# A planner of engine queues gets three more rounds, ranked by deadlines worked out backwards from a plan

## The chip, the core and the metric

The kernel runs on one core of a Trainium2 chip. Work is spread over TensorE (PE in the rows; PEld is its weight load), VectorE (DVE), ScalarE (ACT), GpSimd (POOL) and SyncE (SP), which here issues every DMA. Each engine takes its instructions in the order in which they were written to its queue, and waits at one whose inputs aren't there. The metric is the device time of one execution in microseconds (us); lower is better.

## What is computed

Two layers (DEPTH = 2) of a diffusion trunk, over 640 tokens: 512 latent ones and 128 of context. In each layer one input projection feeds three branches.

```python
h = _rms(x, p['norm_g']) * (1 + scale) + shift          # shift, scale, gate from silu(c) @ w_mod
proj = h @ p['w_in']
...
o_a = _attend(q, k, v)                                  # A: latent attention, low-rank q and kv
...
o_f, s_f = _gdn_chunk(gq, gk, gv, g[:, :, 0], beta[:, :, 0], s0[:, 0])   # B: gated DeltaNet, forward
o_bw, s_b = _gdn_chunk(fl(gq), fl(gk), fl(gv), ...)     #    and backward, summed; 4 heads
...
o_c = _chunk_mlp(cu, cv, p)                             # C: 128-position spatial gating
br = jnp.stack([o_a * jax.nn.silu(z_a), o_b * jax.nn.silu(z_b), o_c * jax.nn.silu(z_c)], axis=2)
yb = jnp.einsum('btnw,nwd->btnd', br, p['w_branch'])
y = jnp.sum(gates * yb, axis=2) @ p['w_o']
x = x + gate * y
```

Branch B needs, for each head and direction, the inverse of a 128x128 unit triangular matrix in each chunk of tokens, and then a scan over the chunks.

## The kernel before

Activations lie feature-major, 128 rows by 640 tokens, handled in halves of 320 columns. The long products are made from three matmuls each: weights and activations are split into a rounded part and a rest (`hi` and `lo` of the weights, `hh0` to `hh7` and `hl0` to `hl7` of the normed input), by `split_w` with one copy on ScalarE and one subtraction on VectorE. `dense` runs 24 such matmuls of 320 columns into one of the two PSUM buffers tagged `dn`, and an evacuation on ScalarE or VectorE then empties it.

The layer is written in program order as: the first blocks of the projection (`begin`, `Side`), the decay and gate vectors, and then four DeltaNet heads (`qkv_head`, `gdn_head`, `inverse`), with the projections of other branches between them (`gelu_block`, `silu_block`, `win`); then attention, then the three branches' products (`branch`), then `w_o`. At the start of the kernel the input `xT` is squared and summed for the norm, while the modulation matrix `w_mod` is loaded in 32 pieces into the buffers tagged `G` and multiplied with `s32`.

`inverse` is a chain of small matmuls on PE (tiles `p` of 32x32 and 64x64) with a copy, a transpose or a product on ScalarE or VectorE between each two: `pa`, `t1`, `pb`, `Y2`, `Y2T`, `pc`, `t2`, `pd`, `pe` and so on. Beside `t2`, the copy on which the next small matmuls hang, ScalarE makes twelve quarter copies of `Y2` and `Y2T` into `Y` and `YT` there.

Nothing of this is issued at once. A `Recorder` takes down every instruction with its engine, its predecessors by the tiles that it reads and writes, and a cost in ns from a table (`cost`). `issue` then calls `best`, which plans, and writes the instructions in the planned order; it fixes each engine's order with added dependencies. So every instruction carries the line of `issue` in the profile (L371 before). The planner, `plan`, is a list scheduler: it steps through time, and an engine that is free takes, of the instructions whose inputs are ready, the one with the lowest `prio`, and goes on to the next in rank only if a buffer that it needs isn't free. `prio` is the place in the program (`op.prio = op.n - self.off`), less 100000 for those recorded under `rec.hp()`, such as weight splits, evacuations and softmax. `slack` makes results count as later by so many ns when PE waits for them. `best` tries the four values of `SLACKS` and keeps the plan with the lowest modelled end.

Of the kernel before, what the change touches and what calls it, by code (L numbers as in the profile page):

```python
# [48 lines left out]
HOP = {"V": 36, "S": 36, "G": 60, "PE": 53, "SP": 60}  # L49
AFTER = {"V": 33, "S": 122, "G": 60}  # L50
SLACKS = (0, 60, 120, 180)
ISSUE = 475
DMA_LAG, DMA_RATE = 1900, 340.0

# [5 lines left out]
class Recorder:  # L60
# [94 lines left out]
    def cost(self, op, outs, ins):  # L155
# [3 lines left out]
        if e == "SP":  # L159
            big = max((x.nbytes() if callable(x.nbytes) else x.nbytes) for x in outs + ins)  # L160
            op.occ, op.lat = ISSUE, big / DMA_RATE
        elif e == "PE":
# [17 lines left out]
        else:  # L180
# [22 lines left out]
            if e == "S" and n == 160 and outs[0].ap[0][1] == 32:  # L203
                op.occ, op.lat = 260, 320

    def best(self):

        plans = []
        for slack in SLACKS:
            self.plan(slack)  # L210
            plans.append((self.total, slack))
        return self.plan(min(plans)[1])

    def plan(self, slack):
        import heapq
# [1594 lines left out]
```

## Time and profile before

| | |
|---|---|
| median of 3 runs | 1681.33 us (1680.39 to 1683.24) |
| the profiled execution, its own time | 1683.82 us |
| its span, first to last instruction | 1681.9 us |
| mean granted TensorE clock | 0.989 of full |
| instructions in the profile | 34993 |
| PE / DVE / ACT busy, share of the span | 97% / 76% / 53% |

The span is what the views divide up; 1.9 us of the execution lie around it. A PE that is busy need not be at full rate: it may run at half its clock, and the ends of its matmuls are modelled.

### The profile page before, as it was taken

Reading aid. Unit: us, or ns where it says so; the run is one execution under the profiler, and the core shown is the slowest. Engines: PE = TensorE matmul, PEld = TensorE weight load, DVE = VectorE, ACT = ScalarE, POOL = GpSimd, SP = SyncE. Lnnn points to the kernel's source line nnn. Section 1 sums busy time; section 2 is a strip of 40 time slices with the busy share of each in tenths; the row PEclk is TensorE's granted clock in tenths of the full one; section 3 lists DMA queues with packets and bytes.
Section 4 is the critical chain, followed back from the end, with each engine's and each line's share of the span. In section 5 each row is a group of like instructions: output and inputs, shape, how many; then the busy total and the mean of one; then the engine's idle time right before and its main releaser. Section 6 shows DMA issues by size and latency. Waiting matters only on the chain. (4 is left out here: it accounts for less than half of the span.)

```text
span 1681.9 us, 34993 instructions
## 1 busy us (share of the span) xinstructions
PE 1636.5 (97%) x13286; PEld 1538.7 (91%) x13286; DVE 1284.8 (76%) x3638; ACT 890.2 (53%) x2201; POOL 16.7 (1%) x100
## 2 busy tenths in 40 slices
PE   6999998999999999999999999989999999999998
PEld 5998988999889989989989989989998899899998
DVE  4898898665655768877988987976656557789898
ACT  3566664554545554434445676646545455545453
POOL 0000000000000000000000000000000000000000
PEclk9999999999999999999989999999999999999999
DMA  9312211222121212555542212212211122113342
GB/s 298 95 56 55 62 58 50 66 69 62 46 60 58 91 51 97 178 185 157 188 156 64 58 42 63 58 50 78 70 52 53 49 64 88 57 65 98 94 161 80
DMA packets 94616, 146.39 MB, mean 87 GB/s; under 512 B 14064, under 2 KB 38000, under 8 KB 94448
## 3 DMA queue, kind: packets, MB, share of 16 engines
q1 hardware_dynamic: 94448, 144.15, 28.0%
q8 instruction: 105, 1.72, 0.4%
q14 instruction: 63, 0.52, 0.1%
HBM read 132.28 MB, written 11.83 MB: 86 GB/s over the span
## 5 line engine op out<-in xcount | busy, mean ns | idle before, releaser
L371 PE MATMUL dn<-hh,hi 128*128 128x320 f32 (+1 forms) x1472 | 469.6, 319 | 4.8 <-ACT hh L371 2.1
L371 PE MATMUL dn<-hl,hi 128*128 128x320 f32 (+1 forms) x1472 | 469.1, 319 | 0.4 <-DVE hl L371 0.3
L371 PE MATMUL dn<-hh,lo 128*128 128x320 f32 (+1 forms) x1472 | 467.9, 318 | 0.0
L371 ACT CAST hi<-raw 128x512 fp32r<-128x512 f32 (+1 forms) x300 | 186.1, 620 | 198.5 <-PE dn L371 101.1
L371 PEld LDWEIGHTS dn<-hh,hi 128*128 128x128 f32 (+1 forms) x1472 | 277.1, 188 | 10.1 <-ACT hh L371 3.1
L371 PEld LDWEIGHTS dn<-hl,hi 128*128 128x128 f32 (+1 forms) x1472 | 277.6, 189 | 3.7 <-DVE hl L371 1.2
L371 PEld LDWEIGHTS dn<-hh,lo 128*128 128x128 f32 (+1 forms) x1472 | 277.5, 189 | 2.9 <-issue 1.0
L371 DVE TENSOR_TENSOR lo<-raw,hi 128x512 fp32r<-128x512 f32 (+1 forms) x300 | 206.5, 689 | 60.3 <-ACT hi L371 57.5
L371 PE MATMUL dn<-qkv,hi 128*128 128x320 f32 x768 | 175.0, 313 | 0.5 <-DVE iv L371 0.5
L371 PEld LDWEIGHTS dn<-qkv,hi 128*128 128x128 f32 x768 | 129.4, 189 | 3.3 <-ACT hi L371 1.6
L371 PE MATMUL dn<-qkv,lo 128*128 128x320 f32 x384 | 119.9, 312 | 0.0
L371 ACT CAST hi<-D 128x512 fp32r<-128x512 f32 x88 | 54.6, 623 | 105.9 <-PE dn L371 51.8
L371 PE MATMUL p<-hh,hi 128*128 128x320 f32 x296 | 92.3, 313 | 0.3 <-ACT hi L371 0.3
L371 PE MATMUL p<-hh,lo 128*128 128x320 f32 x296 | 92.2, 312 | 0.0
L371 PE MATMUL p<-hl,hi 128*128 128x320 f32 x296 | 92.0, 311 | 0.2 <-DVE hl L371 0.2
L371 DVE TENSOR_REDUCE mx<-p 128x1 f32<-128x640 f32 x64 | 52.7, 823 | 48.1 <-PE p L371 48.0
L371 ACT ACTIVATE V<-p,mx,scl 128x640 f32<-128x640 f32 x64 | 56.9, 888 | 60.5 <-DVE mx L371 57.2
L371 PEld LDWEIGHTS dn<-qkv,lo 128*128 128x128 f32 x384 | 72.4, 189 | 0.7 <-issue 0.7
L371 PE MATMUL p<-G,hi 128*128 128x320 f32 x286 | 69.3, 308 | 0.0
L371 ACT ACTIVATE th<-dn 128x320 f32<-128x320 f32 x112 | 48.7, 435 | 38.9 <-PE dn L371 38.2
L371 PEld LDWEIGHTS p<-iv,G 32*32 32x32 f32 (+2 forms) x608 | 34.9, 132 | 36.2 <-issue 33.1
L371 PE MATMUL p<-G,G 128*128 128x512 f32 x128 | 65.7, 595 | 0.0
(350 smaller groups left out, 3484.0 us busy)
## 6 DMA issues: line engine op xcount, KB each, us to landing
raw<-in_w_in SPq DMA_DIRECT2D x212, 256.0 KB, 2.7
G<-in_w_mod SPq DMA_DIRECT2D x96, 256.0 KB, 4.4
raw<-in_w_branch SPq DMA_DIRECT2D x48, 256.0 KB, 2.8
D<-in_w_in SPq DMA_DIRECT2D x32, 256.0 KB, 3.3
ld<-sp SPq DMA_DIRECT2D x16, 320.0 KB, 3.1
raw<-in_w_o SPq DMA_DIRECT2D x20, 256.0 KB, 3.1
G<-in_w_uq SPq DMA_DIRECT2D x16, 192.0 KB, 2.7
D<-in_w_o SPq DMA_DIRECT2D x12, 256.0 KB, 3.6
```

The source lines that it names most:

```text
L371: op.ins = getattr(getattr(nc, ENG[op.eng]), op.meth)(*op.args, **op.kw)
```

## The change

`best` now makes 16 plans. For each of the four slacks it plans once with the ranks of before, and then three times more; each further time the rank of an instruction is its deadline in the plan just made. `deadlines` walks that plan from its end to its beginning: an instruction has to be done before the earliest deadline of those that need its result, or that take over its buffer (`slotdeps`), less a hand-over time, and on PE also before the deadline of the next matmul in PE's order. Of the 16 plans the one with the lowest modelled end is issued. Costs, dependencies, buffers and the instructions themselves stay as they are.

```diff
+ROUNDS = 4
...
+    def deadlines(self, out):
+
+        succ = {op.n: [] for op in out}
+        for op in out:
+            for p in op.preds:
+                succ[p].append(op)
+        for op, nm in self.slotdeps:
+            for u in self.users[nm]:
+                succ[u.n].append(op)
+        latest, after = {}, None
+        for op in reversed(out):
+            end = self.total
+            for s_ in succ[op.n]:
+                lag = 53 if s_.eng != op.eng else op.occ - op.lat if op.eng == "PE" else 33
+                end = min(end, latest[s_.n] - lag)
+            t = end - op.lat - (DMA_LAG if op.eng == "SP" else 0)
+            if op.eng == "PE":
+                if after is not None:
+                    t = min(t, latest[after.n] - max(op.occ, op.ld))
+                after = op
+            latest[op.n] = t
+        return latest
+
     def best(self):
 
+
+        first = [op.prio for op in self.ops]
         plans = []
         for slack in SLACKS:
-            self.plan(slack)
-            plans.append((self.total, slack))
-        return self.plan(min(plans)[1])
+            prio = first
+            for n in range(ROUNDS):
+                for op, p in zip(self.ops, prio):
+                    op.prio = p
+                out = self.plan(slack)
+                plans.append((self.total, slack, n, prio))
+                late = self.deadlines(out)
+                prio = [late[op.n] for op in self.ops]
+        _, slack, _, prio = min(plans, key=lambda x: x[:3])
+        for op, p in zip(self.ops, prio):
+            op.prio = p
+        return self.plan(slack)
```

The instructions are the same ones on every engine; their places move by a few up to some tens. On PE the last fifth of the program and the middle of each layer (the branch products) stay in place; what moves lies at the start, in the part of each layer with the DeltaNet heads, and a little at the border of the two layers. Both layers move alike. Three places follow; in the names, the first number is that of the tile.

PE in the inverse of head 0, layer 0, before: `p2_291` are the matmuls `pc`, `p2_293` and `p2_294` are `pd` and `pe`, which read the copy `t2` (`iv_292`), and `dn_443` is the next block of the projection.

```order
L371 MATMUL p2_291_359<-iv_287_355,G_216_284 32x32 x20
L371 MATMUL p2_293_361<-iv_280_348,iv_292_360 32x32 x20
L371 MATMUL p2_294_362<-iv_292_360,iv_280_348 32x32 x10
L371 MATMUL dn_443_511<-hh0_69_137,hi_438_506 128x320
L371 MATMUL dn_443_511<-hl0_70_138,hi_438_506 128x320
L371 MATMUL dn_443_511<-hh0_69_137,lo_439_507 128x320
L371 MATMUL dn_443_511<-hh1_76_144,hi_438_506 128x320
```

The same place on PE now.

```order
L406 MATMUL p2_291_359<-iv_287_355,G_216_284 32x32 x20
L406 MATMUL dn_443_511<-hh0_69_137,hi_438_506 128x320
L406 MATMUL dn_443_511<-hl0_70_138,hi_438_506 128x320
L406 MATMUL dn_443_511<-hh0_69_137,lo_439_507 128x320
L406 MATMUL dn_443_511<-hh1_76_144,hi_438_506 128x320
L406 MATMUL dn_443_511<-hl1_77_145,hi_438_506 128x320
L406 MATMUL dn_443_511<-hh1_76_144,lo_439_507 128x320
L406 MATMUL p2_293_361<-iv_280_348,iv_292_360 32x32 x20
L406 MATMUL p2_294_362<-iv_292_360,iv_280_348 32x32 x10
```

Six dense matmuls moved in between the small ones that make `pc` and those that read its copy.

ACT at this place before, from the copy `t1` (`iv_285`) to the copy `t2` (`iv_292`): `G_288` and `G_289` are `Y`, `iv_290` is `YT`, and `C_424` is the evacuation of the dense buffers `dn_431` and `dn_432`, which comes only after these rows.

```order
L371 COPY G_289_357<-iv_280_348 32x5x32
L371 COPY iv_290_358<-iv_287_355 32x5x32
L371 CAST hi_601_669<-raw_600_668 128x512
L371 COPY iv_290_358<-iv_287_355 32x5x32 x2
L371 COPY G_288_356<-iv_280_348 32x5x32
L371 COPY G_289_357<-iv_280_348 32x5x32
L371 COPY iv_290_358<-iv_287_355 32x5x32
L371 COPY iv_292_360<-p2_291_359 128x160
```

And now, the whole way from `t1` to `t2`.

```order
L406 COPY iv_285_353<-p2_284_352 128x160
L406 ACTIVATE C_422_490<-C_421_489 128x644
L406 COPY C_424_492<-dn_431_499 128x320
L406 COPY G_288_356<-iv_280_348 32x5x32
L406 CAST hi_441_509<-raw_440_508 128x512
L406 COPY G_288_356<-iv_280_348 32x5x32
L406 COPY iv_290_358<-iv_287_355 32x5x32 x4
L406 COPY C_424_492<-dn_432_500 128x192
L406 COPY C_424_492<-dn_432_500 128x128
L406 COPY G_289_357<-iv_280_348 32x5x32
L406 COPY iv_292_360<-p2_291_359 128x160
```

Five quarter copies and a weight split (`hi_601`) moved behind `t2`; the activation `C_422` and three evacuations, which stood behind it, moved ahead of it.

DVE later in layer 0, where the inverse of head 2 begins, before: `iv_728` is the product `Bm` that the first small matmuls (`p2_729`) wait for, `R_727` its factor `brs`; `ir_691`, `res_692`, `br__693`, `br2_694` and `G_701` belong to head 3, whose inverse comes later; `ld_831` empties the dense buffer `dn_830`.

```order
L371 TENSOR_SCALAR D_595_663<-D_595_663,mv_580_648,R_597_665 128x512
...
L371 SCALAR_TENSOR_TENSOR R_727_795<-br2_462_530,c_m01_6_74,R_727_795 128x5
L371 TENSOR_TENSOR ya4_599_667<-ya4_599_667,D_819_887 128x640
L371 SCALAR_TENSOR_TENSOR ir_691_759<-ssq_686_754,r_689_757 128x5
L371 TENSOR_TENSOR res_692_760<-g_E_155_223,r_689_757 128x5
...
L371 TENSOR_TENSOR G_701_769<-p2_700_768,ir_691_759 128x640
L371 TENSOR_TENSOR iv_728_796<-iv_728_796,R_727_795 128x160
L371 SCALAR_TENSOR_TENSOR ld_831_899<-dn_830_898,lngh_818_886,C_817_885 128x512
```

And now.

```order
L406 SCALAR_TENSOR_TENSOR R_727_795<-br2_462_530,c_m01_6_74,R_727_795 128x5
...
L406 TENSOR_TENSOR iv_728_796<-iv_728_796,R_727_795 128x160
...
L406 TENSOR_SCALAR D_592_660<-D_592_660,mv_580_648,R_597_665 128x512
L406 SCALAR_TENSOR_TENSOR D_819_887<-th_829_897,dn_828_896 128x320
L406 TENSOR_SCALAR D_595_663<-D_595_663,mv_580_648,R_597_665 128x512
L406 SCALAR_TENSOR_TENSOR ld_831_899<-dn_830_898,lngh_818_886,C_817_885 128x512
```

`iv_728` moved from behind head 3's vectors to ahead of the five products that scale `D_583` to `D_595`, and `ld_831` to directly behind them; head 3's vectors and `G_701` moved behind both. PE's matmuls `p2_729` moved with it, in between the last matmuls of the block `dn_828` and those of `dn_830`.

SP's queue at the start: before, `c_cc` and `ident` are issued ahead of the eight loads of `xT`, and the weight loads `raw_59`, `raw_62` and `raw_65` stand among the loads of `w_mod`. Now the `xT` loads come first, `ident`, `b_mod` and `norm_g` come behind the first eight `w_mod` loads, and the three weight loads stand behind nearly all of them; on PE, the matmuls that use `raw_62` and `raw_65` (tiles `p2_74<-...,D_63` and `D_66`) moved behind those of later pieces of the input.

## Rows read from the trace of the kernel before

**Rows 1.** The page: busy time, share and instructions of each engine.

```profile
PE 1636.5 (97%) x13286; PEld 1538.7 (91%) x13286; DVE 1284.8 (76%) x3638; ACT 890.2 (53%) x2201; POOL 16.7 (1%) x100
```

**Rows 2.** What PE waited for, whole span: total us, times, longest us.

```profile
PE p L371 <- DVE C L371: 12.9, 1, 12.9
PE p L371 <- DVE iv L371: 6.1, 4, 2.7
PE p L371 <- ACT iv L371: 5.9, 4, 2.6
```

**Rows 3.** Stretches: length, busy (x instructions) of each engine, clock, DMA share, GB/s.

```profile
0.00:42.00 42.00, 26.92 (x281) 21.31 (x282) 20.13 (x54) 14.98 (x24) 0.71 (x13) 0.96 0.94 299
126.00:168.00 42.00, 39.16 (x455) 36.94 (x454) 35.84 (x121) 28.42 (x85) 0.82 (x10) 0.96 0.21 55
236.00:264.00 28.00, 23.17 (x195) 20.96 (x194) 27.35 (x117) 18.09 (x66) 2.13 (x4) 0.98 0.24 74
256.00:263.00 7.00, 3.65 (x63) 3.14 (x62) 7.00 (x25) 3.13 (x10) 0.00 (x0) 0.98 0.39 123
264.00:276.00 12.00, 12.00 (x227) 10.51 (x226) 4.98 (x14) 6.56 (x20) 0.64 (x1) 0.91 0.09 25
276.00:308.00 32.00, 30.26 (x222) 28.61 (x219) 28.66 (x119) 14.96 (x47) 0.36 (x1) 1.00 0.19 52
840.00:883.00 43.00, 39.97 (x287) 35.10 (x286) 37.85 (x95) 19.75 (x34) 0.51 (x9) 0.88 0.45 152
967.00:1177.00 210.00, 199.74 (x2145) 188.75 (x2144) 168.66 (x610) 129.76 (x401) 5.80 (x25) 0.98 0.20 58
1596.00:1682.00 86.00, 80.22 (x543) 79.29 (x541) 76.21 (x153) 36.42 (x65) 0.00 (x0) 1.00 0.37 121
```

**Rows 4.** PE in time, head 0's inverse: start, length; in brackets idle before.

```profile
141.70 0.55 PE L371 MATMUL p<-iv,G 32*32 32x32 f32 x40
144.82 0.84 PE L371 MATMUL p<-iv,iv 32*32 32x32 f32 x60 [2.58 <-ACT iv L371]
145.91 0.42 PE L371 MATMUL dn<-hh,hi 128*128 128x320 f32 x1 [0.24 <-ACT C L371]
146.16 0.31 PE L371 MATMUL dn<-hl,hi 128*128 128x320 f32 x1
```

**Rows 5.** ACT in time, same place.

```profile
144.48 0.29 ACT L371 COPY iv<-p 128x160 f32<-128x160 f32 x1
144.80 0.74 ACT L371 ACTIVATE C<-C 128x644 f32<-128x644 f32 x1
145.44 0.80 ACT L371 COPY C<-dn 128x320 f32<-128x320 f32 x3
```

**Rows 6.** PE in time, where head 2's inverse begins.

```profile
258.96 0.49 PE L371 MATMUL dn<-C,D 128*128 128x128 f32 x2 [0.56 <-DVE D L371]
262.14 0.55 PE L371 MATMUL p<-iv,iv 32*32 32x32 f32 x40 [2.69 <-DVE iv L371]
262.80 0.63 PE L371 MATMUL dn<-hh,hi 128*128 128x320 f32 x1
```

**Rows 7.** DVE in time, same place.

```profile
258.41 0.50 DVE L371 SCALAR_TENSOR_TENSOR D<-th,dn 128x320 f32<-128x320 f32 x1
261.02 0.83 DVE L371 TENSOR_TENSOR G<-p,ir 128x640 f32<-128x640 f32 x1
261.75 0.33 DVE L371 TENSOR_TENSOR iv<-iv,R 128x160 f32<-128x160 f32 x1
261.98 0.76 DVE L371 SCALAR_TENSOR_TENSOR ld<-dn,lngh,C 128x512 f32<-128x512 f32 x1
```

**Rows 8.** SP and PE in time, the start.

```profile
0.73 0.38 SPq L371 DMA_DIRECT2D c_cc<-in_cc  x1
1.64 3.77 SPq L371 DMA_DIRECT2D ya<-in_xT  x8
26.13 0.35 PE L371 MATMUL dn<-hh,hi 128*48 128x320 f32 x1 [1.75 <-ACT hh L371]
```

## Prediction, made before the changed kernel had run

> **What bounds the kernel now.** I read the page's shares first: PE is busy 97% of the span, DVE 76%, ACT 53% [rows 1]. So nothing that the change does to DVE or ACT counts unless PE stops waiting for it or begins to. The same matmuls are issued before and after; a new order can win only PE's idle time and the time in which PE runs below its full clock. The span of 1681.9 us less 1636.5 of PE work leaves 45.4 us idle, and the second table, by stretches, says where: the start 42.00 − 26.92 = 15.1 us, the part of layer 1 with the DeltaNet heads 210.00 − 199.74 = 10.3, the border of the layers 43.00 − 39.97 = 3.0, the end 86.00 − 80.22 = 5.8 [rows 3]. Layer 0 has the same waits again (the list of waits counts each kind twice, below), so 2 × 10.3 + 15.1 + 3.0 + 5.8 = 44.5 of the 45.4 are placed. The end isn't touched by the change, and at the start one wait of 12.9 us is that for the first input, before any work [rows 2]. What an order can win is therefore mostly the 20.5 us in the two head parts, and the clock there: the mean of 0.98 over 210 us is 210 × 0.02 = 4.2 us per layer, lost where PE runs at 1.2 GHz and not at 2.4. (A mean clock of 0.9 is 0.2 of the time at the lower level, which does half the work, so 0.1 of the time is lost.)
>
> The waits of PE show two large ones in each layer: for DVE's `iv` 6.1 us in four waits, the longest 2.7, and for ACT's `iv` 5.9 in four, the longest 2.6 [rows 2]. Two layers, so per layer one of 2.7 and one of 0.3, and one of 2.6 and one of 0.35. In layer 0 they stand at 262.14 (2.69 us, after which the first matmuls of head 2's inverse run [rows 6]) and at 144.82 (2.58 us, before `pd` and `pe` of head 0's [rows 4]). I take layer 0 as the pattern and count each term twice.
>
> **Head 2's inverse.** Up to 262.14 PE waits for `iv_728`, which DVE makes at 261.75 in 0.33 us, behind `G_701` (261.02, 0.83 us) [rows 7] and head 3's vectors. DVE is full there, 7.00 of 7.00 us from 256 to 263 [rows 3], so its order is what decides. In the new order `iv_728` stands ahead of the five `D` products, and `ld_831` right behind them. The second matters as much: with `p2_729` run early, PE's next dense block has to wait for `ld_831`, which empties its buffer. Its input `dn_830` is complete at 258.96 + 0.49 = 259.45 at the latest [rows 6], and what DVE must still do ahead of it is the product `D_819` (258.41, 0.50 us [rows 7]), the last scaling product, and itself, 0.76 us [rows 7]; I put the dense block at 259.9 and not 262.80 [rows 6]. That gains 2.9; I take 2.8. Bounds: 1.0, if only part of the head start survives (`iv_728` moves by its own place, but `ld_831` comes after all five products and `R_727` is late), and 2.69 + 0.56 = 3.2, all idle time there. What was put off (`G_701` and three small vectors) goes to the next stretch, where DVE has 12.00 − 4.98 = 7.0 us free [rows 3]: that is its cover, and without it head 3's inverse would be late by 0.83 us and more.
>
> After this wait the granted clock is 0.91 over 12.00 us [rows 3], a mix of 1.2 and 2.4 GHz that costs 12 × 0.09 = 1.1 us; before the wait it was 0.98. With the idle time gone I count 1.0 of it as won (0 to 1.1).
>
> **Head 0's inverse.** `pc` ends at 141.70 + 0.55 and PE stands until 144.82, since the copy `t2` that it needs is made on ACT only at 144.48 [rows 4, 5]: quarter copies and a weight split stand ahead of it. Five of the copies and the split now go behind it. Against this, the activation `C_422` (0.74 us) and three evacuations (0.80 together) [rows 5] now go ahead of `pc`'s turn, and DVE puts a product of some 0.7 us (as `ld`, 0.76 [rows 7]) ahead of `iv_287`, which makes `pc` later. So `t2` ends not much later or earlier than before, at about 145.0 against 144.77 by my sum. The gain lies in what PE does meanwhile: six dense matmuls now stand there, which right after the wait start 146.16 − 145.91 = 0.25 us apart [rows 4], and half of that at the other level of the clock: they fill 0.8 to 1.5 us, and I take 0.9, since PE comes to this place at its full clock. The wait of 0.24 behind the small matmuls [rows 4] goes as well, since the evacuations now come first. Net I take 0.9; bounds 0.3 (`t2` later by the whole activation) and 2.0 (`t2` earlier by about a microsecond, besides the fill). From 126 to 168 the clock is 0.96 [rows 3], 42 × 0.04 = 1.7 us; half of it, 0.8 (0 to 1.7), since some idle time stays.
>
> The Trainium skill, in "TensorE: Matmul & The Clock Gate", Part 1, gives ScalarE and VectorE a strict first-in, first-out queue, so that what is written ahead of the copy must finish before it, wanted or not; the wait of 2.58 us agrees, and by that rule alone, without the dense matmuls as a fill, this term would be a loss of some 0.2 and not a gain of 0.9.
>
> **The other waits of the head part.** Of the 10.3 us idle, 42.00 − 39.16 = 2.8 lie in the stretch just told, 28.00 − 23.17 = 4.8 in 236 to 264, 32.00 − 30.26 = 1.7 in 276 to 308 [rows 3]; 0.9 is left for the rest (from unrounded numbers). In that rest stand the two short waits for `iv`, 0.3 and 0.35 [rows 2]; copies and products moved ahead there too, and I take 0.7 (0 to 0.9). In 236 to 264, 4.8 − 2.69 − 0.56 = 1.6 us remain, waits inside a scan chain, which no order shortens much on a DVE that is busy 27.35 of 28.00: 0.3 (−0.5 to 1.0). In 276 to 308 chunks of six dense matmuls now stand between the scan's steps, so that PE has work while ACT and DVE hand over; DVE at 28.66 of 32.00 [rows 3] bounds it: 1.0 of the 1.7 (0 to 1.7).
>
> Per layer: 2.8 + 1.0 + 0.9 + 0.8 + 0.7 + 0.3 + 1.0 = 7.5 us; for two, 15.0. The bounds add up to 0.8 and 11.6 a layer, 1.6 and 23 in all.
>
> **Start.** The loads of `xT` are issued first instead of from 1.64 us on, behind `c_cc` at 0.73 [rows 8]: 0.9 us earlier for the chain that PE's 12.9 us wait for. Against it, `raw_62` and `raw_65` now come behind nearly all of `w_mod`. DMA is busy 0.94 of these 42 us at 299 GB/s [rows 3], so place in the queue is arrival time; the matmuls with these weights filled the time in which PE waits for the next piece of the normed input (1.75 us before 26.13 [rows 8]), and now can't: I charge 1.3. Net +0.4 us (−2 to +2). `c_cc` lands later by eight issues, but its use stands behind the squares of `xT` on ACT; if not, the start pays up to 3.77 us, the time of the `xT` issues [rows 8].
>
> **Border.** Some `G` work and a group of matmuls go ahead into the wait there, and a cast and a copy go ahead of the chain that follows, by up to 1 us; of 3.0 us idle at a clock of 0.88 [rows 3] I count nothing either way (−1.5 to +1).
>
> **Sum.** −15.0 + 0.4 = −14.6, on the execution's own 1683.8 us: 1669.2. That execution lies 2.5 us above the median of the three runs, so against the median 1681.3 − 14.6 = 1666.7: **1667 us**.
>
> **Rivals.** First, *the waits only move*. From 236 to 308 DVE is busy 56.0 of 60.0 us outside the one stretch from 264 to 276 [rows 3]; what is put off to free `iv_728` delays the next thing by as much, and head 0's `t2` is no earlier. Then only the fills count: 0.9 + 0.3 + about 0.5 a layer, no clock, less 0.4 at the start: a gain of 2 to 6, 1675 to 1679. Against it speak the 7.0 us that DVE has free just behind. Chance 0.18. In this kernel `iv` was made only when `G` was done [rows 7], which is what this rival asks of every engine's queue.
>
> Second, on the other side, *head 3 pays*. Its vectors and `G_701` are now behind head 2's start, and head 3's own inverse and scan follow on a full DVE (28.66 of 32.00 [rows 3]). If what is put off, with the `D` products that follow it, outgrows the 7.0 us of room by about 5 us, head 3's first products wait those 5 us unfilled, and the clock falls with them by another 1 to 2 (as after 262.14): 6.5 a layer lost against some 4 still won, +2.5 a layer, 1686. The point from which it decides is `G_701` made later than about 276. Chance 0.05.
>
> Third, *nothing comes of it*: each wait is replaced by its like a few rows on, since the same work hangs on the same chains; within 2 us of 1681. PE's idle list, with its two long waits for single late copies rather than many even ones, speaks against it. Chance 0.07. The forecast, a gain of 6 to 23, has 0.70.
>
> **How the numbers follow.** About 0.2%, 3.4 us, is what a measurement of this kernel can tell from no change, so faster means below 1678. The forecast's cases, 0.70, are all faster, of the first rival two thirds, 0.12: 0.82. The third rival and the rest of the first make 0.13 the same, the second 0.05 slower. The range takes the forecast down to 1658 (all upper bounds) and the first rival up to 1679; outside lie the other two rivals, 0.12, and some 0.05 of tails.
>
> **What would show it.** In the changed trace, PE's waits for `iv` should fall from 12 us to under 5; the wait before `p2_729` should be below 0.5, with the clock behind it at 0.97 or more; before `pd` some 1 to 2 us should remain, behind six dense matmuls; the head part of a layer should be 203 and not 210 us long. PE's first matmul should start about 0.9 us sooner and the dense matmuls on the last pieces of the input about 1 later. The prediction fails if DVE's full stretches only shift, so that waits for `D`, `ld` or `G` grow by what those for `iv` lose, or if the clock in the head part stays at 0.98 with less idle time.

## The result and the profile after

| | before | after |
|---|---|---|
| median | 1682.09 us (4 runs) | 1658.20 us (4 runs) |
| ratio to before | | 0.9864, 95% interval 0.9841 to 0.9887 |
| the profiled execution, its span | 1683.82, 1681.9 us | 1656.81, 1654.9 us |
| PE work; PE idle | 1636.5; 45.4 us | 1623.1; 31.8 us |
| mean clock of the executions | 0.988 to 0.994 (44 runs) | 0.997 to 1.000 (8 runs) |

The kernel is 23 us faster; 1667 was forecast, and 1658.2 lies at the lower edge of the range. (The clocks of before come from the runs beside the experiments; four of the eight runs of after are those of `x_after`, below.) Here is the page of the kernel after, which answers to [rows 1].

```profile
PE 1623.1 (98%) x13286; PEld 1527.4 (92%) x13286; DVE 1277.6 (77%) x3638; ACT 888.6 (54%) x2201; POOL 16.9 (1%) x100
```

The instructions are as many as before; PE's work is nevertheless 13.4 us shorter, and its idle time 13.6. So one half of the 27.0 us between the two spans is idle time; the other is, for the most part, time in which PE ran at 1.2 and not at 2.4 GHz. PE's waits in the kernel after, with the total, the number and the longest:

```profile
PE p L406 <- DVE C L406: 11.3, 1, 11.3
...
PE p L406 <- ACT iv L406: 2.1, 4, 0.6
...
PE p L406 <- DVE iv L406: 1.5, 2, 0.8
```

The waits for `iv`, 12.0 us in [rows 2], are 3.6 here, with none above 0.8. To see where the time went, both traces are cut at the same points of the program. First the kernel before, by stretches (columns as in [rows 3]): the start, then in layer 0 head 0 with what lies around it, the middle of the head part, heads 2 and 3, the beginning of attention; the border; head 0 and heads 2 and 3 of layer 1; the end.

```profile
0.00:86.97 86.97, 71.89 (x635) 63.85 (x636) 59.63 (x163) 38.80 (x84) 1.40 (x25) 0.98 0.64 193
86.97:192.36 105.39, 102.55 (x925) 100.29 (x924) 95.03 (x330) 72.02 (x228) 3.77 (x18) 0.98 0.20 53
192.36:229.96 37.60, 36.64 (x445) 34.56 (x443) 30.54 (x128) 25.64 (x72) 0.17 (x3) 1.00 0.22 65
229.96:326.19 96.23, 89.53 (x977) 82.44 (x975) 77.44 (x298) 54.47 (x175) 3.13 (x6) 0.98 0.20 60
361.70:395.51 33.81, 33.81 (x240) 33.60 (x239) 24.98 (x102) 15.53 (x39) 0.00 (x0) 0.95 0.24 73
799.50:894.17 94.67, 91.14 (x640) 84.14 (x639) 82.73 (x190) 42.94 (x79) 0.85 (x15) 0.95 0.46 156
894.17:1028.01 133.84, 131.26 (x1118) 129.23 (x1116) 120.83 (x396) 87.66 (x269) 4.10 (x24) 0.97 0.20 58
1065.60:1161.67 96.07, 89.34 (x976) 82.50 (x974) 77.67 (x297) 54.53 (x175) 3.13 (x6) 0.98 0.20 59
1615.22:1681.80 66.58, 61.00 (x412) 60.07 (x410) 59.85 (x122) 27.59 (x50) 0.00 (x0) 1.00 0.40 135
```

The same nine stretches of the kernel after.

```profile
0.00:84.88 84.88, 70.57 (x636) 62.51 (x636) 58.51 (x161) 37.96 (x83) 1.39 (x25) 1.00 0.65 197
84.88:187.21 102.33, 101.44 (x924) 99.06 (x923) 93.94 (x331) 71.07 (x226) 3.76 (x18) 1.00 0.18 55
187.21:224.61 37.40, 36.54 (x444) 34.56 (x443) 30.66 (x132) 26.22 (x74) 0.17 (x3) 1.00 0.22 64
224.61:316.19 91.58, 88.77 (x977) 82.10 (x976) 78.07 (x295) 55.74 (x175) 3.14 (x6) 1.00 0.21 62
352.06:385.31 33.25, 32.50 (x240) 32.12 (x239) 24.51 (x102) 15.39 (x39) 0.00 (x0) 1.00 0.23 67
788.73:880.55 91.82, 88.47 (x639) 81.77 (x639) 82.85 (x191) 42.80 (x80) 0.85 (x15) 1.00 0.49 161
880.55:1010.39 129.84, 129.04 (x1117) 126.98 (x1116) 118.63 (x395) 87.02 (x267) 4.10 (x24) 1.00 0.21 59
1047.80:1138.70 90.90, 88.44 (x977) 82.06 (x975) 77.51 (x294) 55.62 (x175) 3.36 (x6) 1.00 0.21 62
1590.32:1654.80 64.48, 60.31 (x412) 60.04 (x410) 59.75 (x122) 27.42 (x50) 0.00 (x0) 1.00 0.42 139
```

Length less PE's work is idle time; the fall of PE's work from one table to the other is mostly the clock. Head 0 in layer 0: 105.39 − 102.33 = 3.1 us won, of which 2.84 − 0.89 = 1.95 is idle time and 1.1 PE's work; in layer 1 4.0, 1.8 idle and 2.2 work. Heads 2 and 3: 4.65 and 5.2 us won, 3.9 and 4.3 of it idle, 0.8 and 0.9 work. The start 2.1 (0.8 idle), the border 2.85 (0.2 idle), the end 2.1 (1.4 idle). Where attention begins 0.6 us were won: PE's work fell by 1.3, and 0.75 us of idle time came in that weren't there. The clock is 1.00 in all nine stretches of after.

### The profile page after: what moved, and what is told of

It reads as the page before. It is cut to its first block, busy times and chain, and to the rows that moved or that the text cites. A ratio compares the mean times of both kernels' runs of the same rounds, so it can differ in the third digit from the quotient of the medians.

```text
span 1654.9 us, 35005 instructions
## 1 busy us (share of the span) xinstructions
PE 1623.1 (98%) x13286; PEld 1527.4 (92%) x13286; DVE 1277.6 (77%) x3638; ACT 888.6 (54%) x2201; POOL 16.9 (1%) x100
## 4 chain that ended last, share of the span: by engine, by line
PE 86%; DVE 7%; ACT 4%; issue 1%; DMA 1%; SPq 0%; DVEq 0%; ACTq 0%
PE dn L406 44%; PE p L406 26%; PE mm L406 16%; DVE C L406 2%; ACT G L406 1%; ACT iv L406 1%; DVE lo L406 1%; DVE G L406 1%; DVE iv L406 1%; DVE R L406 1%; DVE D L406 1%; DVE ya L406 1%; ACT hi L406 1%; ACT C L406 1%; DVE qkv L406 0%
## 5 line engine op out<-in xcount | busy, mean ns | idle before, releaser
L406 PE MATMUL dn<-hl,hi 128*128 128x320 f32 (+1 forms) x1472 | 463.1, 315 | 0.2
L406 ACT COPY V<-p 128x640 f32<-128x640 f32 x64 | 44.3, 692 | 43.2 <-PE p L406 42.2
```

Of the source, the lines that this page charges most:

```text
L406: op.ins = getattr(getattr(nc, ENG[op.eng]), op.meth)(*op.args, **op.kw)
```

## The experiments

A kernel can issue any mixture of the two orders that keeps the dependencies: the two plans are made, and each instruction takes its place from one of them. In the first four kernels, and in `x_heads` further below, the instructions with places in the listed ranges of the plan of before take their places from that of after, on all engines.

```diff
+        a, b = seqs[0], seqs[2]      # plans of before and of after
...
+        at = {op.n: i for i, op in enumerate(a)}
+        to = {op.n: i for i, op in enumerate(b)}
...
+        for i, j in RANGES:
+            new |= {op.n for op in a[i:j]}
+        seq = sorted(a, key=lambda op: (to if op.n in new else at)[op.n])
```

`x_h0`: RANGES = [(853, 2113), (9181, 10754)]

> The order of before everywhere except in the part of each layer around head 0's inverse (in layer 0 from 87 to 192 us of the trace of before, in layer 1 from 894 to 1028), where all engines take the order of after. Theory 1 (each stretch gains by itself what the two traces show as the growth of PE's lead there: 3.4 us in layer 0, 4.4 in layer 1, idle time and clock together): 7.8 us faster than before, about 1674, with no fall of the clock after head 0's wait and the falls at 262, 372, 862, 1098 and 1206 us still there. Theory 2 (the sizes of the prediction: 0.9 + 0.8 a layer): 3.4 faster, about 1678.5. Theory 3 (the clock's falls come by the chance of when a wait lies, so parts do not add up): falls at other places come or go with this edit, and the gain is anywhere from 2 to 14.

`x_h23`: RANGES = [(2630, 3760), (11271, 12400)]

> The order of before except where heads 2 and 3 are set up, inverted and scanned (230 to 326 us and 1066 to 1162 us of the trace of before), where all engines take the order of after. Theory 1: PE's lead grows there by 4.5 us in each layer, so 9 us faster than before, about 1673; the falls at 262 and 1098 us are gone, the others stay. Theory 2 (2.8 + 1.0 + 0.3 + 1.0 a layer, as predicted): 10.2 us faster, about 1672. Theory 3: untouched falls of the clock come or go, gain anywhere from 4 to 16.

`x_edge`: RANGES = [(0, 853), (8267, 9181)]

> The order of before except at the start (to 87 us) and at the border of the layers (799 to 894 us), where all engines take the order of after. Theory 1: the lead grows by 1.9 us at the start and 2.9 at the border, so 4.8 us faster, about 1677; the falls of the clock at 27 and 862 us are gone. Theory 2 (prediction: 0.4 us slower at the start, nothing at the border): about 1682.5. Theory 3: as for the others, from 0 to 10 faster.

`x_rest`: everything but those six ranges.

> The complement: the order of after everywhere except in the stretches of the three kernels x_h0, x_h23 and x_edge, which keep the order of before. Theory 1: the lead grows here by 0.2 in the middle of the head parts, 0.6 and 1.3 where attention begins, 0.9 in layer 1's attention and branches and 2.0 in the last 60 us, together 5.0 us: about 1677, and the falls at 27, 145, 262, 862, 979 and 1098 stay. Theory 2 (prediction: 0.7 a layer in the middle of the head part and nothing else): about 1680.5. Theory 3: the places at 372 and 1206, where PE runs 20 matmuls of one column in a row in both orders, show a fall or none by chance, so this part gains from 1 to 5.

| kernel | median | ratio to before (95%) | that is | by the traces (theory 1) | by the prediction (theory 2) |
|---|---|---|---|---|---|
| `x_h0` | 1675.63 | 0.9963 (0.9951 to 0.9975) | 6.2 us faster | 7.8 | 3.4 |
| `x_h23` | 1669.11 | 0.9927 (0.9915 to 0.9939) | 12.3 | 9 | 10.2 |
| `x_edge` | 1679.72 | 0.9996 (0.9984 to 1.0009) | 0.7 | 4.8 | −0.4 |
| `x_rest` | 1678.39 | 0.9981 (0.9969 to 0.9992) | 3.2 | 5.0 | 1.4 |

The us are the ratio's distance from 1 times 1682. Their sum is 22.4, as good as the whole change. The start and the border gain nothing that can be told from nothing, as predicted, and against the 4.8 us by which the two traces differ there. To see why, all profiles were cut into pieces of 3 us and those with a clock under 0.98 marked; these are the places at which it fell (L0, L1: the layers; lost: the sum over the pieces of 3 us times one less the clock; the last 4 us of each kernel are left out), for these and the later kernels:

| kernel | start | head 0's wait | head 2's wait | attention begins | border | lost, us |
|---|---|---|---|---|---|---|
| before | yes | L0 L1 | L0 L1 | L0 L1 | yes | 18.8 |
| `x_h0` | | | L0 L1 | L0 L1 | yes | 13.6 |
| `x_h23` | yes | L0 L1 | | | yes | 10.2 |
| `x_edge` | yes | L0 L1 | L0 L1 | L0 L1 | yes | 20.5 |
| `x_rest` | | L0 L1 | L0 L1 | L1 | yes | 10.2 |
| `x_heads` | yes | | | L0 | yes | 6.8 |
| after | | | | | | 0.0 |
| `x_after` | yes | | | | yes | 5.1 |
| `d_back` | | L0 L1 | | L0 L1 | yes | 8.5 |
| `d_dup` | yes | | | L0 | yes | 10.2 |
| `r_one` | | | | L0 L1 | yes | 5.1 |
| `i_cols` | | | | L0 L1 | yes | 8.6 |
| `i_keep` | | | | | | 0.0 |

Two kinds of falls stand apart. Where a layer has the long wait of head 0, the clock fell in 10 cases of 10, and without it in none of 16; for head 2's it is 8 of 8 and none of 18. Those at the start (6 of 13), at the border (11 of 13) and where attention begins (15 of 26) come and go between profiles in which that place has the same order; only the border in the order of before, with a wait of 2.2 to 3.6 us for `R`, fell in all five of its profiles. So theory 1 holds for the long waits, theory 3 for the rest; the profile of after happened to have none of them. The next kernel is the same order again.

> The order of after, word for word, once more, to see how much its clock varies. The four parts taken one by one gave 0.37%, 0.73%, 0.04% and 0.19%, in sum 22.4 us. Theory 1 (the gain is made of the parts): about 1659, with a mean clock of 0.997 or more in every execution. Theory 3 (the clock's falls come by chance): single executions with a clock of 0.995 or less and times up to 1668.

It took 1657.81 us (0.9867, 0.9848 to 0.9885), so the result stands; the clock was 0.997 to 1.000. Its profile was the slowest of its four runs (1662.08) and has falls at the start and the border. Of the 5.3 us by which its span is longer than after's, 4.1 are PE's work (1627.2 us) and 1.2 idle time; 0.8 of the latter is one wait at the border for a piece of `w_mod`, 1.03 us long and not 0.19, just ahead of the fall there. PE's rows at the start, first of after, then of `x_after`:

```profile
23.79 0.35 PE L406 MATMUL dn<-hh,hi 128*48 128x320 f32 x1 [1.76 <-ACT hh L406]
...
25.08 0.35 PE L406 MATMUL dn<-hl,hi 128*48 128x320 f32 x1
25.27 0.31 PE L406 MATMUL dn<-hh,lo 128*48 128x320 f32 x1
```

```profile
24.68 0.35 PE L425 MATMUL dn<-hh,hi 128*48 128x320 f32 x1 [1.58 <-ACT hh L425]
...
25.97 0.42 PE L425 MATMUL dn<-hl,hi 128*48 128x320 f32 x1
26.19 0.47 PE L425 MATMUL dn<-hh,lo 128*48 128x320 f32 x1
```

The order is the same and the wait even a little shorter, 1.58 us against 1.76; yet in the second the same matmul takes 0.47 us instead of 0.31. The Trainium skill, in "TensorE: Matmul & The Clock Gate", Part 1, says that the gate looks at PE's activity on a schedule of its own, which isn't tied to the kernel, so that the same program changes over at different points from run to run; these rows agree with that, and don't prove it.

Next, what the six dense matmuls do that now stand in head 0's wait. In `d_back` they go back behind the small ones; in `d_dup` their place is taken by repeats without use.

```diff
+            six = pe[i + 1 : j]          # between pc and pd
...
+            rest = [op for op in seq[:at] if op not in six]
+            seq = rest + six + seq[at:]  # now behind pe
```

```diff
+            for _ in six:                # d_dup, besides the above
...
+                op.kw = dict(first.kw, stop=True)
...
+                seq.insert(seq.index(first), op)
```

> The order of after, but in both layers the six dense matmuls that stand between `pc` and `pd` of head 0's inverse go back behind `pe`, as before; ACT and DVE keep the order of after. Theory 1 (the fill saves its own length, and the wait without it brings the clock's fall back): 0.9 us a layer for the fill and 1.3 for the clock, so 4.4 slower than after, about 1662.5, mean clock 0.998. Theory 2 (the copy `t2` that comes earlier is what saved, the fill is worth little): at most 1 us slower. In the profile PE should stand some 1.5 to 2.0 us ahead of `pd`.

> As d_back, but where the six dense matmuls stood, the first of them runs six more times, its result overwritten by the real one later: PE is as busy in the wait as in after, but the work is of no use. Theory 1 splits the two gains: the clock is held as in after, the fill's length is lost, so 0.9 to 1.5 us a layer slower than after, 1660 to 1661, faster than d_back by about 2.6. Rival (only useful work counts, the clock doesn't hang on this wait): the same time as d_back, or slower, and the same clock.

`d_back` took 1664.39 us (0.9900, 0.9882 to 0.9918), `d_dup` 1661.98 (0.9886, 0.9866 to 0.9906). PE in time in the kernel after, from `pc` by way of `pd` to the next product of 64x64:

```profile
139.99 0.55 PE L406 MATMUL p<-iv,G 32*32 32x32 f32 x40
...
142.17 0.84 PE L406 MATMUL p<-iv,iv 32*32 32x32 f32 x60 [0.55 <-ACT iv L406]
...
144.90 0.32 PE L406 MATMUL p<-iv,G 64*64 64x64 f32 x2
```

The same in `d_back`, and below it the clock over 6 us there:

```profile
140.14 0.55 PE L438 MATMUL p<-iv,G 32*32 32x32 f32 x40
142.32 0.84 PE L438 MATMUL p<-iv,iv 32*32 32x32 f32 x60 [1.62 <-ACT iv L438]
...
147.46 0.32 PE L438 MATMUL p<-iv,G 64*64 64x64 f32 x2
```

```profile
141.00:147.00 6.00, 4.68 (x76) 4.64 (x77) 3.84 (x9) 4.20 (x12) 0.00 (x0) 0.72 0.19 47
```

And in `d_dup`:

```profile
143.26 0.55 PE L451 MATMUL p<-iv,G 32*32 32x32 f32 x40
143.74 1.14 PE L451 MATMUL dn<-hh,hi 128*128 128x320 f32 x6
145.44 0.84 PE L451 MATMUL p<-iv,iv 32*32 32x32 f32 x60 [0.56 <-ACT iv L451]
...
149.05 0.33 PE L451 MATMUL p<-iv,G 64*64 64x64 f32 x2
```

```profile
144.00:150.00 6.00, 5.44 (x99) 4.72 (x100) 3.72 (x9) 4.31 (x13) 0.00 (x0) 1.00 0.19 46
```

In all three the small matmuls of `pd` start 2.2 us after `pc` began; the fill doesn't move them. Without it the wait is 1.62 us and the clock falls to a mean of 0.72 over 6 us; with matmuls of no use it is 0.56 and the clock stays at 1.00. What each is worth shows at the product of 64x64: up to it PE has the same useful matmuls to do in the three kernels, and it starts 144.90 − 139.99 = 4.91 us after `pc` in after, 5.79 in `d_dup` and 7.32 in `d_back`. In layer 1 the three are 4.92, 5.79 and 7.32. So the fill saves 0.9 us a layer, and the clock that it holds 1.5. Together that is 4.8 of the 6.6 us by which `d_back` is slower than `x_after`; the profile of `d_back` has, besides, two falls where attention begins. `d_dup` is 4.2 slower than `x_after`, more than the 1.8 that the missing fill explains; its profile has one fall of the second kind more.

The medians of `d_back` and `d_dup` differ by 2.4 us, as theory 1 has it, but their intervals overlap, and the mean clock of their executions is the same (0.994 to 0.996), as the rival has it. The falls of the second kind hide the difference: at the border the profile of `d_dup` lost 6.8 us, that of `d_back` 1.7. That the repeats hold the clock is shown at the place itself, in both layers; for the time of the whole kernel it isn't.

> One backward pass instead of two: the plan for slack 60 is ranked by the deadlines of the first plan, and issued without a choice among plans. Theory 1 (the deadlines as such make the gain): within 3 us of after, 1656 to 1663. Rival (the gain comes of choosing the best of many different orders): most of it is missing, 1666 to 1680.

```diff
-SLACKS = (0, 60, 120, 180)
+SLACKS = (60,)
...
-        _, slack, _, prio = min(plans, key=lambda x: x[:3])
+        _, slack, _, prio = plans[1]
```

1658.79 us (0.9866, 0.9849 to 0.9884): one backward pass is as good as the pick of sixteen plans. The deadlines themselves make the gain.

Two kernels were to beat after by holding the clock in the places of the second kind. What PE did where attention begins, in the kernel before (the chain of one-column matmuls, then by stretch the 4 us behind it):

```profile
369.45 2.34 PE L371 MATMUL mm<-c_ones,qkv 128*128 128x1 f32 x20
```

```profile
372.00:376.00 4.00, 4.00 (x19) 4.00 (x18) 2.84 (x13) 0.95 (x2) 0.00 (x0) 0.58 0.08 31
```

PE was busy all the time, and the clock fell. `i_cols` breaks this run up, in both layers; `i_keep` also repeats matmuls without use in the waits of the start and the border.

```diff
+            for c, r in zip(cols, [y for y in ys for _ in range(2)]):
+                seq.remove(c)
+                seq.insert(seq.index(r), c)
...
+                    op.args = (first.args[0], first.args[1], full)   # i_keep
+                    op.kw = dict(start=True, stop=True)
...
+                    seq.insert(seq.index(pe[i + back]), op)
```

> The order of after, but where attention begins, in both layers, the twenty matmuls of one column on PE no longer run in a row: a product of 320 columns stands after every four of them. Of the ten profiles taken so far six showed a fall of the clock just there in layer 0 and six in layer 1, with PE busy without a gap. Theory 1 (the run of one-column matmuls is what lets the clock fall): no fall at these two places, about 1 us faster than after on the mean, about 1657, mean clock 0.998 to 0.999. Rival (the fall has its cause earlier, in the waits of the head part): falls there in about half of the cases, no gain.

> As i_cols, and besides, PE repeats matmuls of no use (320 columns, overwritten later) while it waits for the normed input: 10 of them at the start, and at the border of the layers 14 in the long wait and 12 between the products with w_mod ahead of it. Theory 1 (what is left of the clock's falls in after comes from the start, the border and the one-column matmuls, and work of any kind in these places holds the clock): mean clock 0.999 to 1.000 in every execution, 1655 to 1657 with a smaller scatter. Rival (the matmuls of no use come into the way of the chain at the border): falls are gone but the border is longer by up to 12 x 0.13 = 1.6 us, so the same as after. Second rival: the falls stay, and the time is 1658 to 1660.

`i_cols` took 1662.88 us (0.9891, 0.9871 to 0.9911): no faster than after, 4.7 us above it by the medians with intervals that overlap, and the clock fell at both places again. Its PE rows show a new wait ahead of the run, because the one-column matmuls now come sooner than their input:

```profile
360.59 0.61 PE L437 MATMUL mm<-c_ones,qkv 128*128 128x1 f32 x4 [0.52 <-ACT V L437]
361.06 0.40 PE L437 MATMUL p<-D,G 128*128 128x320 f32 x1
361.29 0.50 PE L437 MATMUL mm<-c_ones,qkv 128*128 128x1 f32 x4
```

So it doesn't settle what lets the clock fall there. `i_keep` took 1661.0 us (0.9891, 0.9863 to 0.9918), with a clock of 0.999 in three of four executions and 0.997 in the fourth, and yet it is no faster than after: with the clock at 1.00 up to its last 2 us, its span is 1657.6 us and that of after 1654.9. PE's work on its page is 1627.1 us, 4.0 more than after's, with 36 matmuls more, the repeats:

```profile
PE 1627.1 (98%) x13322; PEld 1531.3 (92%) x13322; DVE 1277.8 (77%) x3638; ACT 889.0 (54%) x2201; POOL 17.2 (1%) x100
```

So there is no net gain. What the repeats themselves cost isn't separated: `i_keep` has the new waits of `i_cols` too, 0.52 us a layer, and against `i_cols`, from which only the repeats tell it apart, its ratio is the same. No kernel here beats after.

The last kernel asks whether the parts add up and what becomes of the clock.

> The stretches of x_h0 and x_h23 together take the order of after, in both layers; everything else keeps that of before, the start, the border, the beginning of attention and the end with it. Theory 1 (the parts add up): 0.37% + 0.73%, so 18.5 us faster than before, about 1663. Theory 2 (the prediction's sizes for these stretches): 3.4 + 10.2 = 13.6 faster, about 1668. Theory 3, on the clock: with the two long waits of each layer gone four falls are gone for certain, worth 5.0 us of PE time, and the mean clock should rise from 0.990 to 0.993 if the other places fall as often as in before, and to 0.997 or more if their falls hang on the first four.

1664.45 us (0.9894, 0.9877 to 0.9911): 17.8 us faster, near the sum of the parts, and above the prediction's 13.6, which the interval (15.0 to 20.7) leaves out. Its clock was 0.994 to 0.995: more than the 0.993 that the four certain falls explain, and less than after's. That after reaches 0.997 to 1.000 isn't explained by any part alone; it stays open.

## Why the prediction was right, and where its sizes were off

The direction and the mechanism were right: the gain came from PE's waits in the head parts, mostly the two long ones, and from the clock behind them. The size was too small: 14.6 us were forecast, and the four parts measured 22.4 together: 2.8 more than forecast at head 0, 2.1 more at heads 2 and 3, 1.8 more in the rest and 1.1 more at the start and the border. That the range held the result is luck: it did so by 0.2 us, and the same order measured again, 1657.81, lies outside. Its end at 1658 is called that of all upper bounds, but leaves out those of the start (2) and the border (1.5); with them it is about 1655. The steps one by one:

- **Head 2's inverse and the scan** (2.8 + 0.3 + 1.0 idle, 1.0 clock a layer). The stretch won 3.9 and 4.3 us of idle time, where 4.1 were predicted, and 0.8 and 0.9 of PE's work, where 1.0 was. The place was a little different: DVE in the kernel after shows `iv_728` early and `ld_831` then waiting for PE, not the reverse,

```profile
249.79 0.32 DVE L406 TENSOR_TENSOR iv<-iv,R 128x160 f32<-128x160 f32 x1
...
255.24 0.75 DVE L406 SCALAR_TENSOR_TENSOR ld<-dn,lngh,C 128x512 f32<-128x512 f32 x1 [0.81 <-PE dn L406]
...
259.54 0.81 DVE L406 TENSOR_TENSOR G<-p,ir 128x640 f32<-128x640 f32 x1
```

  since the forty small matmuls now lie among those of `dn_830`. `G_701`, put off by the change, comes 259.54 − 249.79 = 9.75 us behind `iv_728`, where it stood 0.7 ahead of it [rows 7]; head 3 did not pay for that, and the second rival has nothing for it. `x_h23` measured 12.3 us against 10.2; its profile also lacks the falls where attention begins, which are of the second kind.
- **Head 0's inverse** (0.9 idle and 0.8 clock a layer) is the term that was mis-sized most: 1.95 and 1.8 us of idle time were won, and 1.1 and 2.2 of PE's work, and `x_h0` measured 6.2 us where 3.4 were predicted. The step that failed is "`t2` ends not much later or earlier than before". From PE's start on `pc` to ACT's start on `t2` it was 144.48 − 141.70 = 2.78 us [rows 4, 5]; after, ACT shows

```profile
137.36 0.74 ACT L406 ACTIVATE C<-C 128x644 f32<-128x644 f32 x1 [1.50 <-DVE C L406]
138.01 0.41 ACT L406 COPY C<-dn 128x320 f32<-128x320 f32 x1
...
141.10 0.49 ACT L406 COPY C<-dn 128x192 f32<-128x192 f32 x2
141.61 0.32 ACT L406 COPY G<-iv 32x160 f32<-32x160 f32 x1
141.84 0.28 ACT L406 COPY iv<-p 128x160 f32<-128x160 f32 x1
142.14 1.66 ACT L406 COPY G<-iv 32x160 f32<-32x160 f32 x5
```

  with PE's `pc` begun at 139.99, so 1.85. The activation and the first evacuation ran ahead of `pc`, not between it and `t2`: the prediction counted their whole length into a stretch that they had left before it began. So both gains came, 0.9 us of idle time from `t2` and 1.62 − 0.56 = 1.06 from the fill, and before `pd` 0.55 us of wait remain where 1 to 2 were foretold. The sum also reads the 0.25 us between the first two dense matmuls [rows 4] as the lower clock; the clock of before is 1.00 there, the next ones start 0.15 us apart, and it falls only at 146.6. And the clock came back whole, not by half, since the 0.55 us that PE still waits there did not bring it down.
- **The middle of the head part** (0.7): idle 0.96 before and 0.86 after. The two short waits were replaced by others; 0.1 was won.
- **Start and border** (0.4 lost, nothing): measured together as 0.7 us faster with an interval that holds both; right within it. The first matmul starts 12.91 − 11.26 = 1.6 us sooner, not 0.9, and idle time falls by 0.8 and 0.2 us in all.
- **The end** ("isn't touched by the change") was wrong: PE's rows stay in place, but what it waits for does not, and 1.4 us of idle time went there. That isn't chance: in the last 66.6 us PE is idle for 4.3 to 4.4 us in all eight profiles that don't keep the order of before there, and for 4.9 to 5.8 in the five that do.
- **The clock.** In the two profiles PE's work fell by 13.4 us, nearly all of it by the clock, and 3.6 were forecast, in the heads alone. Of the rest some came by chance in these two executions, as `x_after` shows; the mean clock, 0.990 over the 44 runs of before against 0.997 to 1.000, says that not all of it did.

The first rival (waits only move) and the third (nothing comes of it) fall with `x_heads`.

## What to carry to other kernels

Where a saturated engine makes another wait, look at what stands ahead of the one instruction that is waited for, and count only that part of it which runs after its input is there. A wait of PE that brings the clock down costs about as much again behind it (here 1.5 us behind 1.62); filling it with matmuls that were due anyway returned both, filling it with repeats of no use only the clock, and 36 such repeats at other places made the kernel no faster. Before a gain is explained place by place from one profile of each kernel, take a second one of the same order: here 5 us of difference came and went without any change.

## What the runs showed of the chip that was not expected

The clock fell with PE busy without a gap: 4.00 of 4.00 us at 0.58, behind 2.34 us of twenty one-column matmuls, at the same place in 15 of 26 layers. And one and the same order had a span of 1654.9 us with no fall and of 1660.2 with two; PE's work makes up 4.1 of the 5.3 us between them.
